# The S5 maps of a four-layer decoder on one core: other products on GpSimd, a layout made by transfers within DRAM, and loads of one megabyte

## The chip, the cores and the metric

The kernel runs on one core of one Trainium2 chip. The metric is the device time of one execution in microseconds (us). In the text, PE is TensorE, DVE is VectorE, ACT is ScalarE, POOL is GpSimd and SP is SyncE, as in the profile.

## The reference

256 tokens of 1024 channels pass four layers. Each layer is `h += rmsnorm(mixer(rmsnorm(h)))` and then `h += rmsnorm(mlp(rmsnorm(h)))`. The mixers are a gated MLP over chunks, a causal pooling, a latent attention and, in the last layer, S5, which the change concerns. All is float32.

```python
def s5_mixer(h, lam_re, lam_im, log_dt, b_re, b_im, c_re, c_im, d_skip, w_glu_a, w_glu_b):
    u = h.reshape(B_, S, S5_GROUPS, S5_GROUP_CH)          # 64 groups of 16 channels
    ...                                                    # ab = exp(lam dt), f = (ab - 1) / lam, complex
    bb = f * b                                             # 64 states x 16 channels per group
    bu = einsum('bsgc,gpc->bsgp', u, bb)
    x = scan(x = ab * x + bu)                              # over the tokens, complex
    y = einsum('bsgp,gcp->bsgc', x_re, c_re) - einsum('bsgp,gcp->bsgc', x_im, c_im) + d_skip * u
    y = gelu(y)
    return (y @ w_glu_a) * sigmoid(y @ w_glu_b)
```

## The kernel before

The eight sublayers (gated MLP, Mlp 0, pooling, Mlp 1, attention, Mlp 2, S5, Mlp 3) run one after the other, in blocks of 128 tokens. Every weight is split into two float32r parts, and a float32 product is three products of parts on PE (the helper at L296). SP loads the weights in pieces of 1 MB into three places called `raw`, and ACT (L338) and DVE (L339) split them into eight places called `w`. The order of the instructions on each engine is made by a scheduler that works on the program as it is traced.

**S5** works on chunks of 8 tokens, of which there are 32. Four matrices per group do the work: *f* takes a chunk's inputs to the state (`into`), *m* takes the inputs of a chunk to its outputs (`within`), the states between chunks are scanned on DVE (`scan`), and *e* takes the states to outputs (`out`). What depends on parameters only is made beside layers 1 to 3 by `Tables`, in 16 steps ("chunks of the maps") of two pairs of groups, and it goes to DRAM. S5 then loads these maps: four tiles of 16 groups for each of *f*, *m* and *e*, in `raw` and `w` places, followed by the two GLU weights.

**How the maps are made.** For each of the 16 steps POOL makes the products for *f* with the states in the rows (`ft`), and those for *e*. PE multiplies `ft` by the output matrices (`cb`), which gives *m* by lags between tokens (`pf<-ft,cb`, L296), and it transposes `ft` (L1676), so that the inputs stand in the rows. ACT takes both out of PSUM (L1664, L1678). Every second step PE transposes the lags (L1671), and DVE adds the skip term (`gs`, L1672). POOL issues the stores `d_f` and `d_e` of every step. At the end it stores `gs` to `d_g` 15 times (L1650), at places among zeros written earlier, so that one run of 512 B in `d_g` is a row of *m*.

**How they are loaded.** `load_map` (L1240) loads a tile of *m* by eight DMAs of 128 KB, and `load_out` (L1247) one of *e* by four DMAs of 256 KB. Both read runs of 512 B, on SP's queue, which is also the weights' queue. The *f* tiles are loaded by one DMA each (L113).

**The residual before S5.** S5 takes its tokens in another order. At the end of the attention `reorder` (L444) stores the two blocks of h to `d_h` (L451) and loads them back (L453), all on POOL's queue, behind the maps' last stores. The first readers of the loaded h are the sums of squares on ACT that give the norm factors of Mlp 2 (`junk<-h`, L352). They are wanted only at the end of Mlp 2, but ACT works in order.

Of the kernel before, what the change touches and what calls it, by code (L numbers as in the profile page):

```python
# [9 lines left out]
F32 = mybir.dt.float32  # L10
# [28 lines left out]
N_MAPS = 2  # L39
# [41 lines left out]
class Weights:  # L81
    """The weights in the order of their use, loaded and split ahead of it.

    A weight is the sum of two float32r parts, exactly; a piece is up to 1024 columns of them."""
# [34 lines left out]
    def skip_plain(self):  # L119
        """Past the plain tiles, of which those ahead are loaded where there is a place."""  # L120
# [8 lines left out]
    def ready(self, clock):  # L129
        """Whether the next piece can be split without a long wait for its place."""  # L130
# [34 lines left out]
    def take(self):  # L165
        """The next tile: its pairs, or itself where it is plain."""
# [12 lines left out]
    def free(self, n):  # L179
        """The last use of the next n pieces is emitted."""  # L180
# [9 lines left out]
class Core:  # L190
    """What the sublayers share: memory, the order of emission, norms and splits."""
# [40 lines left out]
    def chain(self):  # L232
        """A chain of short instructions, which the splits traced later don't get in between."""
# [6 lines left out]
    def after(self, first):  # L240
        """Instructions issued after those of first."""
# [6 lines left out]
    def behind(self):  # L248
        """Instructions that wait for the end of the last chain on their engine."""
# [8 lines left out]
    def tick(self, us):  # L258
        """The tensor engine got us of work: emit what runs beside it."""
# [21 lines left out]
    def run(self, units, side=()):  # L281
        """Emits the units (work of the tensor engine, us), and each of side (us, work) at its time among them."""
# [24 lines left out]
    def keep_warm(self, us, after=None):  # L307
        """Holds the tensor engine's clock up over a wait: us of products of zeros, after an instruction."""
# [9 lines left out]
    def acc(self):  # L318
        """[128 tok, 1024] in two banks."""
# [12 lines left out]
    def split(self, src, hi, lo, gain=None):  # L332
        """hi + lo = src, or src gain with [128, 1] of it."""
# [10 lines left out]
    def warm(self, func):  # L344
        """Has the table of func loaded."""
# [1443 lines left out]
```

## Time and profile before

| | |
|---|---|
| Time, median of 3 runs | 1138.8 us |
| The three runs | 1137.75, 1138.8, 1146.0 us |
| Span of the profiled execution (the only time listed for it) | 1139.8 us |
| PE, DVE, ACT, POOL busy | 90%, 64%, 49%, 30% of the span |
| Mean granted clock of PE | 0.955 |
| DMA | 213.84 MB, mean 188 GB/s |

The span is the time from the first to the last instruction of the one execution that was profiled, and it stands 1 us above the median of the runs. A busy share is an average over eight sublayers, so the stages that the change touches are read one by one: the making of the maps (about 215 to 580 us), the reordering of h (about 620 to 670 us) and S5 (about 818 to 935 us).

### The profile page before, as it was taken

The page shows a single profiled execution, that of the slowest core. Times are in us where ns is not written, and L with a number is a line of the kernel's source. Part 1 is how long each engine was busy: PE and PEld are TensorE (multiplying, and loading weights), DVE is VectorE, ACT ScalarE, POOL GpSimd, SP SyncE. Part 2 cuts the span into 40 slices and gives each one's busy share as a digit, 9 for nine tenths or more (in the row PEclk, how much of TensorE's full clock was granted, in tenths as well). Part 3 has the DMA queues.
Part 4 walks back from the last instruction along what each step waited for, and adds up shares of the span by engine and source line. Part 5 has one row for each costly group of instructions (what it writes and reads, how often), then busy time and mean ns, then how long its engine had stood idle before and what let it go on. Part 6 is the DMA issues. An engine that isn't in the chain of part 4 may idle for free.

```text
span 1139.8 us, 18030 instructions
## 1 busy us (share of the span) xinstructions
PE 1029.9 (90%) x7180; PEld 900.4 (79%) x7181; DVE 734.3 (64%) x1133; ACT 555.9 (49%) x841; POOL 343.8 (30%) x514
## 2 busy tenths in 40 slices
PE   7898999999589999997899969999962998999994
PEld 6886989997479888886688859989842787899984
DVE  5779999665686555657865655656574377645552
ACT  6956464454465434534565454545320466444541
POOL 4001002756898887889820100000000000000000
PEclk9999999999799999998899989999985799999998
DMA  9667476653565565545670966455599355555431
GB/s 330 219 222 265 167 250 204 220 184 112 189 236 164 207 206 183 171 146 174 212 220 27 253 190 215 165 206 179 178 176 264 113 179 190 185 184 199 171 112 37
DMA packets 93763, 213.84 MB, mean 188 GB/s; under 512 B 6272, under 2 KB 25984, under 8 KB 93168
## 3 DMA queue, kind: packets, MB, share of 16 engines
q1 hardware_dynamic: 83256, 182.73, 49.8%
q0 software_dynamic: 9872, 29.38, 8.4%
q8 instruction: 56, 0.92, 0.3%
q10 hardware_dynamic: 552, 0.59, 0.1%
q14 instruction: 27, 0.22, 0.1%
HBM read 197.53 MB, written 15.14 MB: 187 GB/s over the span
## 4 chain that ended last, share of the span: by engine, by line
PE 56%; POOL 14%; DMA 11%; issue 9%; DVE 6%; ACT 3%; SPq 0%; DVEq 0%; POOLq 0%; ACTq 0%
PE acc L296 29%; PE mm L296 25%; DMA w<-d_g 3%; DMA h<-d_h 2%; DMA raw<-in_a_w_in 2%; DVE w L339 2%; DMA d_e<-e 2%; POOL tmp L1530 1%; POOL tmp L1527 1%; POOL e L1531 1%; ACT junk L352 1%; POOL e L1528 1%; POOL ft L1531 1%; DVE w L337 1%; POOL ft L1528 1%
## 5 line engine op out<-in xcount | busy, mean ns | idle before, releaser
L339 DVE TENSOR_TENSOR w<-raw,w 128x1024 fp32r<-128x1024 f32 (+3 forms) x308 | 382.5, 1272 | 181.6 <-ACT w L338 180.1
L296 PE MATMUL acc<-w,h1hi 128*128 128x512 f32 (+2 forms) x1824 | 414.2, 350 | 23.6 <-ACT h1hi L338 12.4
L338 ACT ACTIVATE w<-raw 128x1024 fp32r<-128x1024 f32 (+3 forms) x308 | 313.2, 1044 | 243.1 <-PE acc L296 134.7
L296 PE MATMUL mm<-zhi,w 128*128 128x256 f32 x1920 | 357.3, 285 | 3.7 <-DVE s L820 2.3
L296 PEld LDWEIGHTS acc<-w,h1hi 128*128 128x128 f32 (+1 forms) x1824 | 252.5, 180 | 75.5 <-issue 14.4
L296 PEld LDWEIGHTS mm<-zhi,w 128*128 128x128 f32 x1920 | 303.3, 192 | 8.7 <-issue 2.8
L296 PE MATMUL mm<-zlo,w 128*128 128x256 f32 x960 | 273.0, 285 | 0.0
L296 PE MATMUL acc<-w,h1lo 128*128 128x512 f32 (+1 forms) x656 | 253.8, 390 | 1.3 <-DVE h1lo L339 1.3
L296 PEld LDWEIGHTS mm<-zlo,w 128*128 128x128 f32 x960 | 184.6, 192 | 2.3 <-issue 1.2
L296 PEld LDWEIGHTS acc<-w,h1lo 128*128 128x128 f32 x656 | 123.7, 188 | 28.5 <-DVE h1lo L339 2.3
L628 DVE TENSOR_TENSOR s<-s 128x512 f32<-128x512 f32 x56 | 42.0, 749 | 52.4 <-ACT s L627 52.4
L339 DVE TENSOR_TENSOR h1lo<-s,h1hi 128x512 fp32r<-128x512 f32 x60 | 51.2, 856 | 23.4 <-ACT h1hi L338 23.4
L627 ACT ACTIVATE s<-mm 128x512 f32<-128x512 f32 x56 | 33.3, 595 | 64.9 <-PE mm L296 63.2
L338 ACT ACTIVATE h1hi<-s 128x512 fp32r<-128x512 f32 x60 | 45.3, 756 | 25.3 <-DVE s L628 23.5
L1279 POOL MEMSET h1hi<- 128x32 f32 x2 | 0.3, 157 | 181.8 <-PE acc L296 181.8
L401 DVE TENSOR_TENSOR t<-acc,bc 128x512 f32<-128x512 f32 x28 | 19.0, 686 | 39.2 <-PE acc L296 39.2
L296 PE MATMUL mm<-w,zhi 128*128 128x512 f32 x128 | 40.2, 395 | 4.3 <-DVE zlo L339 3.8
L352 ACT ACTIVATE junk<-acc 128x512 bf16<-128x512 f32 x28 | 16.6, 594 | 53.6 <-DVE t L401 52.8
L296 PE MATMUL acc<-w,zhi 128*128 128x512 f32 (+2 forms) x128 | 38.3, 382 | 1.8 <-ACT w L336 1.8
L296 PE MATMUL pf<-ft,cb 128*32 128x128 f32 x128 | 20.8, 302 | 20.0 <-ACT f L1678 7.9
L352 ACT ACTIVATE junk<-h 128x512 bf16<-128x512 f32 x32 | 20.1, 628 | 26.4 <-DMA h<-d_h 16.6
L296 PEld LDWEIGHTS mm<-w,zhi 128*128 128x128 f32 x128 | 23.5, 188 | 10.0 <-DVE zlo L339 4.8
(279 smaller groups left out, 1153.1 us busy)
## 6 DMA issues: line engine op xcount, KB each, us to landing
raw<-in_w_up SPq DMA_DIRECT2D x64, 1024.0 KB, 5.4
raw<-in_w_down SPq DMA_DIRECT2D x64, 1024.0 KB, 5.1
bc<-in_norm_g POOLq DMA_DIRECT2D x15, 512.0 KB, 5.0
raw<-in_a_w_in SPq DMA_DIRECT2D x7, 1024.0 KB, 8.0
raw<-in_a_w_out SPq DMA_DIRECT2D x4, 1024.0 KB, 4.8
d_e<-e POOLq DMA_DIRECT2D x16, 256.0 KB, 3.9
d_f<-f POOLq DMA_DIRECT2D x16, 256.0 KB, 2.8
raw<-in_c_w_o SPq DMA_DIRECT2D x4, 1024.0 KB
```

The source lines that it names most:

```text
L296: return self.nc.tensor.matmul(out, lhsT, rhs, start=start, stop=stop)
L337: return i, nc.vector.scalar_tensor_tensor(lo, src, gain, hi.bitcast(F32), op0=ALU.mult, op1=ALU.subtract)
L338: i = nc.scalar.activation(hi, src, AF.Copy)
L339: return i, nc.vector.tensor_tensor(out=lo, in0=src, in1=hi.bitcast(F32), op=ALU.subtract)
L352: self.nc.scalar.activation(self.junk[:, 0:x.shape[-1]], x, AF.Square, scale=scale, bias=shift, accum_out=ss[:, i:i + 1])
L401: nc.vector.tensor_tensor(tn, zn, gn, op=ALU.mult)
L627: nc.scalar.activation(s, state[f], AF.Relu)
L628: nc.vector.tensor_tensor(s, s, s, op=ALU.mult)
L1527: eng.tensor_tensor(t, xi, yi, op=ALU.mult)
L1528: eng.tensor_tensor(out[0], out[0], t, op=ALU.subtract)
L1530: eng.tensor_tensor(t, xr, yi, op=ALU.mult)
L1531: eng.tensor_tensor(out[1], out[1], t, op=ALU.add)
```

## The change

POOL now makes *f* directly with the inputs in the rows. For this the powers of the decay must lie along a row, the same for the 16 channels. A new function `spread` computes them on DVE (six operations), has PE transpose them (four transposes), ACT copy them, and POOL store them to `d_pw` and copy them within DRAM to `d_pb`, by eight DMAs of 512 KB. Each step of the maps then loads its part of `d_pb` (`pb`) and the input matrices in that layout (`bt`), 256 KB each. The transposes of `ft` and of the lags are gone, with the copies behind them.

The lags are now products of `cb` and *e*, for two steps together, in four strips of 32 columns of PE. They come out as `[128, 128]`, ACT copies them, and `place` on POOL puts them, with zeros and the skip term, into rows that are stored to `d_lag`. When all steps are done, POOL issues four DMAs that copy *e* from `d_out` to `d_e` and eight that copy the lags from `d_lag` to `d_m`. Each is DRAM to DRAM, in runs of 512 B, 4 MB for each of the two. S5 loads *m* and *e* by one DMA of 1 MB per tile, as it loaded *f* before. The zeros of `d_g` and the 15 stores to it are gone. `N_MAPS`, the buffers of `e` and `cb` (before: of `ft` and `cb`), goes from 2 to 3. The rest of the diff takes out comments.

```diff
-N_MAPS = 2
+N_MAPS = 3
...
-        for c in range(4):
-            add(None, plain=True, ahead=True, shape=(16, 128), load=lambda t, c=c: self.load_map(t, c))
-        for c in range(4):
-            add(None, plain=True, ahead=True, shape=(16, 128), load=lambda t, c=c: self.load_out(t, c))
+        for maps in (k.d_m, k.d_e):
+            for c in range(4):
+                add(maps[:, 16 * c:16 * c + 16], plain=True, ahead=True)
...
+    def spread(self):
...
+        for n, (x, y, op) in enumerate(((fr, fi, ALU.subtract), (fi, fr, ALU.add))):
+            nc.vector.tensor_tensor(pw[:, n], turned(pr), wide(x), op=ALU.mult)
+            nc.vector.tensor_tensor(tmp[:, n], turned(pi), wide(y), op=ALU.mult)
+            nc.vector.tensor_tensor(pw[:, n], pw[:, n], tmp[:, n], op=op)
...
+            for n in range(4):
+                nc.tensor.transpose(ps[:, sl(n)], flat[:, sl(n)], k.ident)
+            nc.scalar.activation(s, ps, AF.Copy)
...
+        for i in range(8):
+            src = self.d_pw[:, i].rearrange("r h m -> r (h m)").partition_broadcast(16)
+            nc.gpsimd.dma_start(out=self.d_pb[16 * i:16 * i + 16].rearrange("l r h m -> l r (h m)"), in_=src)
...
     def maps(self):
...
-            self.cmul([v4(ft[:, r]) for r in range(2)], (wide(ov, 0), wide(ov, 1)), (pw(pr, last), pw(pi, last)), v4(tmp))
...
+            nc.gpsimd.dma_start(out=bt.rearrange("p r s m -> p (r s m)"), in_=a["k_bt"][ch])
+            nc.gpsimd.dma_start(out=pb.rearrange("p r s m -> p r (s m)"), in_=self.d_pb[:, :, ch])
...
+            nc.gpsimd.dma_start(out=self.d_out[:, qs], in_=e[:, :, :, 1:9].rearrange("p q r i c -> p q r (i c)"))
+            if made is not None:
+                self.place(lg, *made)
+                made = None
+            f = self.small("f", 4, 2, 64)
+            self.cmul([f[:, :, r] for r in range(2)], (pb[:, 0], pb[:, 1]), (bt[:, 0], bt[:, 1]), tmp.rearrange("p (s m) -> p s m", s=4))
+            nc.gpsimd.dma_start(out=k.d_f[:, 4 * ch:4 * ch + 4], in_=f.rearrange("p s r m -> p s (r m)"))
...
+            if ch % 2:
+                with k.tc.high_priority(offset=-LATER):
+                    made = ch // 2, self.lags((before, (cb, e)))
...
-                nc.gpsimd.dma_start(out=k.d_g[e, :, :, w + 3, o], in_=self.gs[16 * i:16 * i + 16])
...
+        for i, s in enumerate(TOKEN):
+            w = self.d_lag.rearrange("n (g c) f -> c (n g) f", c=16)[:, :, 256 * (s // 4) + 32 * (3 - s % 4):][:, :, 0:128]
+            nc.gpsimd.dma_start(out=k.d_m[16 * i:16 * i + 16], in_=w)
+        for r in range(2):
+            for g in range(2):
+                nc.gpsimd.dma_start(out=k.d_e[64 * r:64 * r + 64, g:64:2], in_=self.d_out[64 * g:64 * g + 64, :, r])
...
-                nc.tensor.transpose(ps[:, sl(2 * r + q)], ft[:, r, sl(q)], k.ident)
...
+    def place(self, lg, n, t):
...
+        nc.gpsimd.tensor_copy(v[:, 0, 0:4, 1], t[:, 1:8:2])
+        nc.gpsimd.tensor_copy(v[:, 0, 4:7, 1], t[:, 2:7:2])
+        for e in range(2):
+            nc.gpsimd.tensor_copy(v[:, e, 4:7, e], t[:, 1:6:2])
+        x = self.small("skip", 16)
+        nc.gpsimd.tensor_scalar(x, self.mask, self.skip[:, n:n + 1], None, op0=ALU.mult)
+        for e in range(2):
+            nc.gpsimd.tensor_tensor(v[:, e, 3, e], t[:, 0], x, op=ALU.add)
+        nc.gpsimd.dma_start(out=self.d_lag[n], in_=lg)
```

The scheduler orders the engines anew. On SP, the loads of S5 (`d_f`, `d_g` or `d_m`, and `d_e` are the maps in DRAM) stand so, before with a minus and now with a plus:

```order
 L113 DMA w<-d_f 128x2048
-L1240 DMA w<-d_g 16x16x128 x32
-L1247 DMA w<-d_e 64x8x128 x12
+L113 DMA w<-d_m 128x2048 x4
+L113 DMA w<-d_e 128x2048 x3
 L113 DMA raw<-in_d_w_glu_b 128x2x1024 x3
-L1247 DMA w<-d_e 64x8x128 x4
+L113 DMA w<-d_e 128x2048
 L113 DMA raw<-in_d_w_glu_b 128x2x1024
```

The order of the tiles is the same; 48 DMAs have become eight.

On POOL, before, the end of the maps and the reordering of h (`h_113` and `h_114` are the two blocks, `bc` are gains of norms, `d_tab` the frames of the scan):

```order
L1640 DMA d_e<-e 128x512
L328 DMA bc<-in_norm_g 128x1024
L1650 DMA d_g<-gs 1024x1x16 x15
L1679 DMA d_f<-f 128x512
L451 DMA d_h<-h_113 128x1024
L328 DMA bc<-in_norm_g 128x1024
L451 DMA d_h<-h_114 128x1024
L328 DMA bc<-in_norm_g 128x1024
L453 DMA h_113<-d_h 128x1x1024
L453 DMA h_114<-d_h 128x1x1024
L1260 DMA t<-d_tab 128x1024 x3
```

And now (`h_117` and `h_118` are the blocks):

```order
L1672 DMA d_e<-d_out 2048x128 x3
L1699 DMA d_lag<-lg 128x512
L451 DMA d_h<-h_117 128x1024
L1659 DMA d_f<-f 128x512
L328 DMA bc<-in_norm_g 128x1024
L451 DMA d_h<-h_118 128x1024
L328 DMA bc<-in_norm_g 128x1024
L1669 DMA d_m<-d_lag 1024x1x128 x8
L453 DMA h_117<-d_h 128x1x1024
L453 DMA h_118<-d_h 128x1x1024
L1246 DMA t<-d_tab 128x1024 x3
```

The eight copies to `d_m` stand between the stores of h and its loads, and the copies to `d_e` before the stores.

On ACT, before, the first readers of the loaded h among the work of Mlp 2 (`L599`, `L600` and `L627` are its activations, `h1hi` their high parts, `w<-raw` splits of weights):

```order
L599 ACTIVATE s<-mm 128x512
L338 ACTIVATE w<-raw 128x1024
L600 ACTIVATE s<-s 128x512
L352 ACTIVATE junk,ss<-h_113 128x512 x2
L352 ACTIVATE junk,ss<-h_114 128x512
L371 ACTIVATE sq<-v 128x1
L352 ACTIVATE junk,ss<-h_114 128x512
L338 ACTIVATE h1hi<-mm 128x32x16
```

And now:

```order
L338 ACTIVATE h1hi<-mm 128x32x16
L627 ACTIVATE s<-mm 128x512
L338 ACTIVATE h1hi<-s 128x512
L338 ACTIVATE w<-raw 128x1024 x2
L627 ACTIVATE s<-mm 128x512
L338 ACTIVATE h1hi<-s 128x512
L338 ACTIVATE w<-raw 128x1024 x4
L627 ACTIVATE s<-mm 128x512
L352 ACTIVATE junk,ss<-h_117 128x512 x2
L338 ACTIVATE h1hi<-s 128x512
```

The readers have moved behind the third activation at L627, which stood third behind them before.

## Rows read from the trace of the kernel before

**Rows 1.** The page, part 1, busy time of PE.

```profile
PE 1029.9 (90%) x7180; PEld 900.4 (79%) x7181; DVE 734.3 (64%) x1133; ACT 555.9 (49%) x841; POOL 343.8 (30%) x514
```

**Rows 2.** Timeline of SP: start, length, DMAs issued.

```profile
818.93 28.21 SPq L1240 DMA_DIRECT2D w<-d_g  x32
```

**Rows 3.** DMA queues, 818 to 850 us: packets, MB, share of 16 engines.

```profile
q1 hardware_dynamic: 8699, 5.18, 106.0%
```

**Rows 4.** DMA from 860 to 880 us, GB/s in slices of 0.5 us.

```profile
GB/s 266 258 210 202 217 287 219 223 243 231 258 215 256 369 418 426 442 377 418 401 418 418 410 442 410 368 318 202 202 206 252 243 246 216 145 223 346 172 205 287
```

**Rows 5.** Chain of waits, 800 to 935 us: start, length, what.

```profile
821.97 7.38 DMA w<-d_g
...
873.03 5.85 issue
...
897.67 36.33 PE acc L296 x160
```

**Rows 6.** Timeline of DVE in S5: start, length, work, idle before.

```profile
837.13 0.42 DVE L1277 TENSOR_TENSOR h1lo<-mm,t 128x256 f32<-128x256 f32 x1 [0.84 <-PE mm L1296]
...
852.43 0.42 DVE L1277 TENSOR_TENSOR h1lo<-mm,t 128x256 f32<-128x256 f32 x1 [2.85 <-PE mm L1296]
...
864.84 0.85 DVE L1277 TENSOR_TENSOR h1hi<-s 64x248 f32<-64x248 f32 x2
...
890.91 2.36 DVE L339 TENSOR_TENSOR w<-raw,w 128x1024 fp32r<-128x1024 f32 x2 [17.95 <-ACT w L338]
```

**Rows 7.** POOL from 350 to 545 us: busy, mean ns, idle before.

```profile
L1531 POOL TENSOR_TENSOR e<-e,tmp 128x256 f32<-128x256 f32 x9 | 11.5, 1281 | 0.6
...
L1526 POOL TENSOR_TENSOR ft<-bo,pr 128x256 f32<-128x256 f32 x9 | 7.8, 867 | 0.7 <-PE pf L1676 0.5
...
L1526 POOL TENSOR_TENSOR bo<-bo,v 128x32 f32<-128x32 f32 x9 | 4.6, 515 | 12.8 <-DMA bo<-in_k_bc 12.8
```

**Rows 8.** Stores of e, L1640: ns min/median/max, first and last start.

```profile
L1640 POOL DMA_DIRECT2D d_e<-e x15: 542/601/606, 237.4 to 561.9; - x15
```

**Rows 9.** What PE waited for, 225 to 635 us: total, times, longest.

```profile
PE pf L296 <- ACT f L1678: 7.9, 1, 7.9
PE pf L296 <- POOL ft L1528: 6.5, 2, 5.2
```

**Rows 10.** Timeline of PE: four transposes of ft, one of lags.

```profile
562.77 0.27 PE L1671 MATMUL pf<-ident,lags 128*128 128x128 f32 x1
...
563.88 0.60 PE L1676 MATMUL pf<-ident,ft 128*128 128x128 f32 x4
```

**Rows 11.** Timeline of POOL, reordering of h.

```profile
621.65 0.55 POOL L451 DMA_DIRECT2D d_h<-h  x1 [41.31 <-DVE h L405]
...
636.39 0.53 POOL L451 DMA_DIRECT2D d_h<-h  x1 [4.25 <-DVE h L405]
...
640.51 1.40 POOL L453 DMA_DIRECT2D h<-d_h  x2 [2.38 <-DMA d_h<-h]
```

**Rows 12.** DMA queue of POOL, 637 to 641 us.

```profile
q0 software_dynamic: 248, 0.95, 65.3%
```

**Rows 13.** DMA queue of POOL, 564 to 580 us.

```profile
q0 software_dynamic: 494, 1.27, 40.1%
```

**Rows 14.** Both DMA queues, 645 to 655 us.

```profile
q0 software_dynamic: 523, 1.32, 99.0%
q1 hardware_dynamic: 41, 0.08, 5.9%
```

**Rows 15.** Timeline of ACT in Mlp 2.

```profile
661.26 0.63 ACT L352 ACTIVATE junk<-h 128x512 bf16<-128x512 f32 x1 [14.34 <-DMA h<-d_h]
...
686.09 0.60 ACT L627 ACTIVATE s<-mm 128x512 f32<-128x512 f32 x1 [3.19 <-PE mm L296]
```

**Rows 16.** Windows, 660 to 665 us: busy by engine, PE clock, DMA.

```profile
660.00:665.00 5.00, 0.00 (x0) 0.00 (x0) 0.21 (x1) 1.47 (x5) 0.00 (x0) 0.63 0.88 304
```

**Rows 17.** What PE waited for, 600 to 720 us.

```profile
PE acc L296 <- ACT h1hi L338: 10.9, 2, 10.2
```

More of the change, by code (lines that the diff above doesn't have):

```diff
@@ L1413, in __init__ @@
         k.d_f = k.dram.tile([128, 64, 128], F32, name="d_f")
-        k.d_e = k.dram.tile([128, 16, 2, 2, 128], F32, name="d_e")
-        k.d_g = k.dram.tile([2, 16, 64, 8, 2, 16], F32, name="d_g")
+        k.d_m = k.dram.tile([128, 64, 128], F32, name="d_m")
+        k.d_e = k.dram.tile([128, 64, 128], F32, name="d_e")
+        self.d_pw = k.dram.tile([2, 8, 16, 256], F32, name="d_pw")
+        self.d_pb = k.dram.tile([128, 2, 16, 256], F32, name="d_pb")
+        self.d_lag = k.dram.tile([8, 128, 512], F32, name="d_lag")
+        self.d_out = k.dram.tile([128, 32, 2, 128], F32, name="d_out")
     def small(self, name, *shape):
@@ L1549, in recurrence @@
         self.mask = load("k_mask", 16)
-        self.skip = load("d_skip", 64)
-        zero = self.wide()
-        nc.gpsimd.memset(zero, 0.0)
-        for n in range(4):
-            part = self.k.d_g.rearrange("b c g w o e -> (b c g) (w o e)")[512 * n:512 * n + 512]
-            nc.gpsimd.dma_start(out=part.rearrange("(p n) f -> p (n f)", p=128), in_=zero)
+        self.skip = load("d_skip", 8)
         v = [self.small(f"v{n}", 32) for n in range(6)]
@@ L1604, in recurrence @@
         yield 0
+        yield from self.spread()
         dec = self.wide().rearrange("p (q j) -> p q j", j=32)
@@ L1633, in maps @@
                 hs = slice(64 * g, 64 * g + 64)
-                nc.gpsimd.tensor_copy(cv[hs, 0, :, g], bv[hs, 2])
-                nc.gpsimd.tensor_scalar(cv[hs, 1, :, g], bv[hs, 3], -1.0, None, op0=ALU.mult)
-            e = self.small("e", 2, 2, 128)
-            first = slice(0, 8)
-            self.cmul([e[:, :, r].rearrange("p q (i c) -> p q i c", c=16) for r in range(2)], (wide(bv, 2), wide(bv, 3)), (pw(pr, first), pw(pi, first)), v4(tmp))
-            nc.gpsimd.tensor_scalar(e[:, :, 1], e[:, :, 1], -1.0, None, op0=ALU.mult)
@@ L1640, in maps @@
-            nc.gpsimd.dma_start(out=k.d_e[:, ch], in_=e)
+                nc.gpsimd.tensor_copy(cb[hs, :, :, g], ov[hs])
+            wide = lambda n: bv[:, n, :, None, :].to_broadcast([128, 2, 8, 16])
+            pw = lambda t: t[:, qs, 0:8, None].to_broadcast([128, 2, 8, 16])
+            self.cmul([e[:, :, r, 1:9] for r in range(2)], (wide(2), wide(3)), (pw(pr), pw(pi)), tmp.rearrange("p (q i c) -> p q i c", q=2, c=16))
+            nc.gpsimd.tensor_copy(e[:, :, :, 0], bv[:, 2:4].rearrange("p n q c -> p q n c"))
@@ L1641, in maps @@
             yield MAPS_US
-            with k.tc.high_priority(offset=-LATER):
-                self.turned(ch, cv, ft)
+            if ch % 2:
+                with k.tc.high_priority(offset=-LATER):
+                    made = ch // 2, self.lags((before, (cb, e)))
+            before = cb, e
             yield 0
-        for i in range(8):
-            lag = 7 - TOKEN[i]
-            at = [(0, lag, 0), (1, lag, 1)] if lag < 4 else []
-            at += [(0, lag - 4, 1)] if lag else []
-            for e, w, o in at:
-                nc.gpsimd.dma_start(out=k.d_g[e, :, :, w + 3, o], in_=self.gs[16 * i:16 * i + 16])
+        self.place(lg, *made)
@@ L1673, in turned @@
-        ps = k.pf.tile([128, 512], F32, name="pf")
-        for q in range(2):
-            for r in range(2):
-                nc.tensor.transpose(ps[:, sl(2 * r + q)], ft[:, r, sl(q)], k.ident)
-        f = self.small("f", 4, 128)
-        nc.scalar.activation(f.rearrange("p g (r m) -> p r g m", r=2), ps.rearrange("p (r g m) -> p r g m", r=2, g=4), AF.Copy)
-        nc.gpsimd.dma_start(out=k.d_f[:, 4 * ch:4 * ch + 4], in_=f)
+        for r in range(2):
+            for n, (cb, e) in enumerate(pairs):
+                for q in range(2):
+                    k.mm(ps[sl32(2 * n + q), 0:128], cb[:, r, q].rearrange("p g c -> p (g c)"), e[:, q, r, 0:8].rearrange("p i c -> p (i c)"), r == 0, r == 1)
```

70 lines of the change are left out of this document (31 added, 39 removed).

## The prediction

> **What bounds the kernel now.** The page gives PE 90% of the span [rows 1], so the first question in each stage is what PE waits for when it does not run. I read the profile in this order: the waits by engine, then the chain of waits of the two stages in which PE stands longest, then the queues behind them.
>
> The first stage is S5. SP issues the 32 loads of *m* over 28.21 us [rows 2]. In that stretch the weights' queue fills the DMA engines, a share of 106% of them, but moves only 5.18 MB in 32 us, 162 GB/s [rows 3]. Some 20 us later, on the same queue, slices of half a microsecond reach 418 to 442 GB/s while a GLU weight is loaded [rows 4]. So this is not a full memory but many short runs. The chain of waits shows what it costs: from 821.97 us it goes through loads of *m*, then through gaps of over 5 us ("issue") before PE's products with *e*, and the dense projection begins only at 897.67 us [rows 5]. The scan on DVE does not set that end: it runs from 837.13 to 865.69 us and stands only 2.85 us in between [rows 6]. After it DVE waits, 17.95 us the last time, for weights that come late.
>
> The second stage is the reordering of h. POOL issues the loads at 640.51 us [rows 11], ACT gets h at 661.26 us after 14.34 us of waiting [rows 15], and PE stands 10.2 us [rows 17]; its clock falls to its lower level in that stretch (0.63 mean over 5 us) [rows 16].
>
> The third is the making of the maps beside layers 1 to 3. PE is mostly busy there; it waits for the maps' own steps 7.9 and 6.5 us in all [rows 9].
>
> **A, making the maps.** Gone from PE are 64 transposes of `ft`, 16 times four at 0.60 us or 9.6 us [rows 10], eight of the lags at 0.27 us, about 2 us [rows 10], and the waits for *f* and `ft`. Added are four transposes. The lag products stay 64, in narrower strips. PE is the engine that sets the pace between those waits, so some 9 us of this would count on the path, the rest being hidden in the waits. ACT and DVE lose 16 evictions and eight sums and gain six small operations, which lie beside PE's work: I cost them at nothing, and it stays so unless DVE's work for `spread` delays a norm.
>
> But PE can only get ahead as far as POOL does. A step on POOL keeps its twelve wide operations, of 0.87 us (product) to 1.28 us (sum) [rows 7]. It gains two loads at 0.6 us each [rows 8], one small copy, and in every second step `place`, seven small operations and a store. It loses two small operations and half a skip product. With 0.5 us for a small operation [rows 7] that is 1.2 + 0.5 + 2.1 - 1.25 = about +2.5 us. Before, the stores of *e* come every 23.2 us over 14 intervals (237.4 to 561.9 us) [rows 8], longer waits included; 2 us of that I put down to those longer waits. So I take about 23.5 us after. The first *f* also starts late, since it waits for the powers. `spread`'s transposes stand in PE's order where the trace has about 250 us, then come `d_pw`, 4 MB of copies to `d_pb` and the load of `pb`. At 2.75 to 5 us per MB (below) that is 272 to 285 us. With *e* of the second step some 14 us later and 14 more steps, the last *e* is ready at 615 to 628 us. PE wants it about 8 us ahead of the store of the second block of h, 636.39 us before [rows 11], and 9 us earlier if it has gained those: at about 620. So 0 to 8 us of the gain are lost again. **A = -4 us**, from -9 to +12, where the upper end is 1.5 us per step that POOL is slower than I think.
>
> **B, the reordering of h.** This is the price of the layout in DRAM. The 8 MB of copies to `d_e` and `d_m` go into POOL's queue ahead of the loads of h. Behind them on POOL wait only h, the scan's frames (not wanted before S5) and two gains. What a megabyte costs there no row of before shows, since no DRAM to DRAM copy ran. The nearest rows of POOL's queue bound it. Without company, 0.95 MB took 65.3% of 4 us: 2.75 us per MB of the engines' time [rows 12]. The 15 stores of lags, in short runs, took 40.1% of 16 us for 1.27 MB: 5.05 us [rows 13]. The load of h, whose neighbouring rows lie 32 KB apart in DRAM, took 99% of 10 us for 1.32 MB: 7.5 us [rows 14]; in that time the weights' queue got 0.08 MB. The 512-byte runs of the old S5 loads make 6.5 us [rows 3]. I take 5.05, the row of POOL's queue with short runs, and keep 2.75 and 7.5 as ends.
>
> [...]
>
> The copies can start when the last *e* is stored, about 625 us. At 5.05 us per MB they hold the engines 40 us if alone, about 55 beside the weights, so to about 680, and h lands at about 684. When is it wanted? ACT's readers of h have moved behind the third L627. Before, that stood at 686.09 us [rows 15], after some 12.6 us of standing and slow clock. So it is wanted at about 673, or 670 with A, and PE has work for 6 us more. PE then stands about 11 us instead of 10.2, plus the clock's 2, and some 4 us go where the weights' queue gets too little: **B = +4 us**. At 2.75 h lands by about 655 and nothing waits: -12. At 7.5 the copies end at 685 or later and the weights stop, with at most 7 MB in their places (some 38 us of work): PE stands about 30 us, +20.
>
> **C, S5.** The maps' loads become eight of 1 MB, in runs as long as those of `d_f`. At 300 to 400 GB/s 8 MB need 20 to 27 us from 818.3 us, so *m* is there by about 834 and *e* by 848 (the last tile waits for its place, not for time). Then nothing in `within` or `out` waits for a transfer, and DVE's scan sets the end: it starts at 837.13 as before and, without the 2.85 us [rows 6], ends at 862.8. All splits of the GLU weights on DVE stand behind it in its new order. Five splits at 1.2 us [rows 6] and two of activations lie ahead of the low parts that the projection needs, so it runs densely from about 870.5 instead of 897.67 us [rows 5]. That would be -27. If the loads run at 250 GB/s, the last tile of *e* comes near 872 and the gain is 18. **C = -25 us**, from -18 to -28. The projection itself takes its 36.33 us as before [rows 5], and what follows moves with it.
>
> **Sum.** Against the profiled execution: 1139.8 - 4 + 4 - 25 = 1114.8. That execution lies 1 us above the median, which I leave in the rounding: 1115 us.
>
> **The rivals.** *No wait for h.* If the copies cost 2.75 us per MB, PE stands nowhere for h: 1139.8 - 4 - 12 - 25 = 1099. For it: plain transfers on this queue do it [rows 12]. Against: both ends are DRAM and the runs are short.
>
> *The copies crowd out h and the weights.* This is the one that ends slower. Place: POOL's queue from 625 us until h lands. It costs PE everything past about 676 us, and it decides where the copies take over 10 us per MB: then 8 MB end at 705, PE restarts at about 712, stands 36 with 4 more for weights and clock, and the 29 us of A and C are eaten. At 15 us per MB, twice the slowest row, they end at 745 and the time is about 1139.8 - 29 + 65 = 1176. For it speaks [rows 14], where 1 MB of h with its 32 KB step took nearly all engines and left the weights 0.08 MB. Against: no row shows 10. A milder form, 7.5 us per MB, gives 1139.8 - 4 + 20 - 25 = 1131.
>
> *GpSimd comes late.* If a step takes 25 us instead of 23.5, the last *e* comes at 650 us, PE waits some 20 to 30 us for the lag products that stand in its order, though h's own wait then falls into it: 1139.8 + 12 - 3 - 18 = 1131.
>
> *The loads gain nothing.* S5 stays as long as it is and the time is 1139.8 - 4 + 4 = 1140. The scan's end at 865.69 [rows 6], 32 us ahead of the projection, and the waits for `w<-d_g` in the chain [rows 5] speak against it. [...]
>
> **How the numbers follow.** A measurement of this kernel can tell about 1% from no change, that is 11.4 us, so faster ends at 1127 and slower begins at 1150. Forecast (1103 to 1127) 0.44, faster. No wait for h 0.20, faster. Copies at 7.5 us per MB 0.08, same. Copies past 10 us per MB 0.14, slower. GpSimd late 0.10, same. Loads gain nothing 0.04, same. So faster 0.64, same 0.22, slower 0.14. The range goes down to 1094 (no wait for h, with A and C at their good ends less a little) and up to 1150, where the slower rival begins; outside lie that rival and a few hundredths below.
>
> **What would show it.** In the changed profile I expect: no load in S5's chain of waits, SP's maps issued in under 10 us, the scan's end at about 863 less the shift before it, the projection right behind it. At the reordering: the copies to `d_m` landing 40 to 55 us after the first copy to `d_e`, an ACT wait for `h<-d_h`, PE idle there 8 to 15 us. In the maps: no `f<-pf`, steps of about 23.5 us on POOL, PE waits for `e` or `cb` of a few microseconds near the end. The forecast is wrong if PE stands over 30 us between 630 and 720 us, if POOL's last map comes after 645 us, or if the projection of S5 begins more than 15 us behind the scan.

## The result

The changed kernel takes 1121.99 us in the median of four runs (1119.85 to 1123.67), the kernel before 1141.32 us in four runs beside them. The ratio is 0.9833, with a 95% interval of 0.9802 to 0.9864: faster, by 19 us. The forecast was 1115 us. The profiled executions differ as much as the medians do, 1139.8 us against 1120.5 us, so their traces can be set side by side. Each trace is cut here at three places that both kernels have: the first block of h after layer 3, the start of S5 (the 34 products of zeros that PE makes ahead of its first products, line 296 on `pf`), and the dense projection of S5.

| | before | after | moved by |
|---|---|---|---|
| first block of h added (DVE `h`, line 405) | 619.92 | 619.73 | -0.2 |
| start of S5 (PE `pf`) | 825.76 | 823.04 | -2.5 more |
| dense projection (PE `acc` x160) | 897.67 | 877.56 | -17.4 more |
| end of the span | 1139.8 | 1120.5 | +0.8 more |

So in this pair of traces terms A and B together brought some 3 us, where they were forecast to cancel, and C brought 17.4 instead of 25. How far one pair can be trusted is taken up with the experiments. PE is busy for 91% of the span, where it was 90% [rows 1].

**S5.** The timeline of SP of the kernel after (start, length, DMAs issued), answering to [rows 2], and the DMA view from 815 to 860 us, answering to [rows 3] and [rows 4]; its first line has slices of 1.1 us, its second the weights' queue with packets, MB and share:

```profile
816.20 5.08 SPq L113 DMA_DIRECT2D w<-d_m  x4
821.64 1.68 SPq L113 DMA_DIRECT2D w<-d_e  x3
...
840.42 0.34 SPq L113 DMA_DIRECT2D w<-d_e  x1
```

```profile
GB/s 0 138 328 430 444 408 430 444 408 430 444 411 397 317 433 408 422 451 408 422 408 419 411 397 426 422 422 441 441 277 51 15 0 0 15 0 0 15 0 0
...
q1 hardware_dynamic: 2112, 12.58, 68.4%
```

The 28.21 us of issuing *m* became 5.08 us, and the queue that gave 162 GB/s with full engines runs at over 400 GB/s in nearly every slice until everything is there at about 848 us. The chain of waits shows what is left, answering to [rows 5], and the timeline of DVE the start and the end of the scan, answering to [rows 6]:

```profile
823.04 7.50 PE pf L296 x34
...
844.79 4.30 issue
849.08 1.93 PE acc L1331 x128
851.01 1.80 issue
...
877.56 36.33 PE acc L296 x160
```

```profile
834.41 0.42 DVE L1263 TENSOR_TENSOR h1lo<-mm,t 128x256 f32<-128x256 f32 x1 [0.84 <-PE mm L1282]
...
859.37 0.85 DVE L1263 TENSOR_TENSOR h1hi<-s 64x248 f32<-64x248 f32 x2
```

No load stands in the chain any more. But it doesn't go through the scan either: it goes along PE, a batch of products and a gap ("issue": PE waits for nothing that the profile shows), again and again, and ends 17 us behind the scan. The timeline of PE (start, length, work, idle before) shows the batches more closely:

```profile
852.81 1.94 PE L1331 MATMUL acc<-w,zlo 128*32 128x32 f32 x128 [1.80 <-issue]
856.54 1.19 PE L1331 MATMUL acc<-w,zlo 128*32 128x32 f32 x73 [1.79 <-issue]
857.53 0.95 PE L296 MATMUL acc<-w,h1hi 128*32 128x32 f32 x55
860.14 1.94 PE L296 MATMUL acc<-w,h1hi 128*32 128x32 f32 x127 [1.67 <-issue]
```

From 842 us on a gap comes after every 128 products (transposes counted), also where a batch runs over the border from one map to the next: 73 of the map `m` and 55 of the map `e` make 128. A product has a weight load beside it (256 products and 255 loads from 852 to 860 us), so that is 256 instructions of PE.

**The maps and h.** The timeline of POOL, answering to [rows 8] and [rows 11]: the first *f*, the last three stores of *e*, and the second block of h:

```profile
269.72 0.72 POOL L1516 TENSOR_TENSOR f<-pb,bt 128x256 f32<-128x256 f32 x1 [3.74 <-DMA pb<-d_pb]
...
576.59 0.82 POOL L1653 DMA_DIRECT2D d_out<-e  x1
...
598.71 0.83 POOL L1653 DMA_DIRECT2D d_out<-e  x1
...
612.60 0.82 POOL L1653 DMA_DIRECT2D d_out<-e  x1
...
645.02 0.54 POOL L451 DMA_DIRECT2D d_h<-h  x1 [12.09 <-DVE h L405]
```

PE's waits from 225 to 720 us (total, times, longest), answering to [rows 9] and [rows 17], the rows of over 3 us for `t` (what the norms give) and for *e*:

```profile
PE mm L428 <- DVE t L418: 16.1, 3, 8.9
PE pf L296 <- POOL e L1518: 12.1, 6, 5.4
PE mm L428 <- DVE t L1041: 4.6, 2, 3.7
...
PE pf L296 <- POOL e L1652: 3.2, 1, 3.2
```

The wait for h is gone, and one of 8.9 us for the norm ahead of Mlp 2 stands in its place. The DMA view from 625 to 665 us (queues; then issues with KB each and median us to landing), answering to [rows 12] to [rows 14], and the timeline of ACT, answering to [rows 15], show why:

```profile
q0 software_dynamic: 2661, 9.86, 67.8%
q1 hardware_dynamic: 2060, 5.14, 34.3%
...
d_m<-d_lag POOLq DMA_DIRECT2D x8, 512.0 KB, 13.8
...
raw<-in_w_up SPq DMA_DIRECT2D x3, 1024.0 KB, 14.5
```

```profile
640.38 1.06 ACT L338 ACTIVATE w<-raw 128x1024 fp32r<-128x1024 f32 x1 [7.50 <-DMA raw<-in_w_up]
641.35 0.19 ACT L371 ACTIVATE sq<-v 128x1 f32<-128x1 f32 x1
...
686.87 0.63 ACT L352 ACTIVATE junk<-h 128x512 bf16<-128x512 f32 x1 [2.91 <-DMA h<-d_h]
```

POOL's queue, most of it the copies, took 67.8% of 40 us for 9.86 MB, 2.75 us per MB (0.678 x 40 / 9.86), and h came in time. Yet they held up a weight of Mlp 2: it took 14.53 us from its issue at 625.77, where the page has 5.5 as the median of 64. ACT stood 7.50 us for it, with the norm's small operation `sq` queued behind; DVE, PE and the second store of h waited in turn. PE's clock fell to 0.50, where [rows 16] has 0.63 (windows; the last three columns are clock, DMA share and GB/s):

```profile
640.00:645.00 5.00, 0.00 (x0) 0.00 (x0) 3.42 (x8) 3.21 (x5) 0.00 (x0) 0.50 1.02 412
645.00:650.00 5.00, 4.52 (x17) 4.06 (x18) 4.14 (x6) 1.79 (x3) 4.30 (x7) 0.50 1.03 406
```

### The profile page after: what moved, and what is told of

Its sections match the earlier page's. It is cut to its first block, busy times and chain, and to the rows that moved or that the text cites. A ratio compares the mean times of both kernels' runs of the same rounds, so it can differ in the third digit from the quotient of the medians.

```text
span 1120.5 us, 17841 instructions
## 1 busy us (share of the span) xinstructions
PE 1020.5 (91%) x7112; PEld 898.2 (80%) x7113; DVE 741.5 (66%) x1131; ACT 546.2 (49%) x818; POOL 377.2 (34%) x588
## 4 chain that ended last, share of the span: by engine, by line
PE 59%; POOL 17%; DVE 9%; DMA 6%; issue 4%; ACT 4%; SPq 0%; DVEq 0%; POOLq 0%; ACTq 0%
PE acc L296 29%; PE mm L296 27%; DVE w L339 3%; POOL tmp L1520 2%; DMA raw<-in_a_w_in 2%; POOL tmp L1517 2%; DMA raw<-in_w_down 2%; DMA raw<-in_w_up 1%; DMA d_f<-f 1%; ACT w L338 1%; ACT junk L352 1%; DVE h L405 1%; PE pf L296 1%; POOL f L1516 1%; POOL e L1652 1%
## 5 line engine op out<-in xcount | busy, mean ns | idle before, releaser
L627 ACT ACTIVATE s<-mm 128x512 f32<-128x512 f32 x56 | 33.4, 596 | 72.6 <-PE mm L296 70.6
L339 DVE TENSOR_TENSOR h1lo<-s,h1hi 128x512 fp32r<-128x512 f32 x60 | 54.0, 901 | 21.4 <-ACT h1hi L338 21.4
L296 PE MATMUL mm<-w,zhi 128*128 128x512 f32 x128 | 42.8, 417 | 2.0 <-DVE zlo L339 1.5
L428 PE MATMUL mm<-ident,t 128*128 128x128 f32 x86 | 14.7, 312 | 24.5 <-DVE t L418 19.9
L428 PEld LDWEIGHTS mm<-ident,t 128*128 128x128 f32 x86 | 11.4, 159 | 27.7 <-issue 26.0
L328 POOL DMA_DIRECT2D bc<-in_norm_g x15 | 8.3, 556 | 75.0 <-DVE t L401 25.2
## 6 DMA issues: line engine op xcount, KB each, us to landing
raw<-in_a_w_in SPq DMA_DIRECT2D x7, 1024.0 KB, 10.5
```

What stands on the lines that cost most here:

```text
L296: return self.nc.tensor.matmul(out, lhsT, rhs, start=start, stop=stop)
L339: return i, nc.vector.tensor_tensor(out=lo, in0=src, in1=hi.bitcast(F32), op=ALU.subtract)
L428: self.nc.tensor.transpose(ps[:, k * 128:(k + 1) * 128], z[:, k * 128:(k + 1) * 128], self.ident)
L627: nc.scalar.activation(s, state[f], AF.Relu)
```

## The experiments

Two questions: what in the loads of S5 was worth 17 us, and what held the rest back (C); and what the copies cost ahead of S5 (A, B). The theory for C was that short runs made the old loads slow; the rival, first put when the trace of after was read, that PE's instructions come too slowly where its products are small. Each experiment's ratio is taken to runs of the kernel before on the same chip (their medians are 1138.69 to 1140.82 us). Profiles of kernels with the same work ahead of S5 start S5 at times up to 10 us apart, so for S5 the stage's own length is compared: from PE's first `pf` in S5 to the end of the span. It is 314.0 us before and 297.5 after. Other traces show how far to trust one such length: with the loads of after it is 294.1 to 296.3 us in the three runs on the copies below (`b_`), but with the old loads 307.5 us in `h_before_late`.

### Loads alone: c_bigloads

The kernel before, its maps in S5 loaded by one DMA per megabyte, all of them from `d_f`, so that *m* and *e* are not the right ones:

```diff
-        for i, s in enumerate(TOKEN):
-            src = self.k.d_g[s // 4, :, 16 * c:16 * c + 16, 3 - s % 4:7 - s % 4].rearrange("c g w o e -> c g (w o e)")
-            self.nc.sync.dma_start(out=t[16 * i:16 * i + 16], in_=src)
+        self.nc.sync.dma_start(out=t, in_=self.k.d_f[:, 16 * c:16 * c + 16])
```

> The kernel before, in which each tile of m and e for S5 is loaded by one DMA of 1 MB from d_f (long runs), so that the products of S5 use other numbers; the making of the maps, the 15 stores to d_g and the reordering of h stay as before. Theory: the long runs alone give the gain that the changed kernel shows in S5, where the dense projection came 17 us earlier against the stage's own start; so 16 to 20 us faster than before, with h's wait of about 14 us on ACT unchanged and gaps of 1.7 to 2.5 us after every 128 small products on PE, no longer 3 to 6 us. Rival: the gain needs the new making of the maps (fewer waits ahead of S5), then less than 8 us.

1126.79 us, ratio 0.9885 (0.9838 to 0.9932), 13 us where 16 to 20 were expected. The stage is 295.8 us long, 18 shorter than before: the loads alone give all that S5 gained in the change, and the new way of making the maps has no part in it. The gaps on PE are the same as after. PE's waits from 815 to 905 us, of before, of after and of `c_bigloads`:

```profile
PE acc L1345 <- issue: 18.8, 5, 5.2
PE acc L296 <- issue: 11.2, 4, 5.9
```

```profile
PE acc L1331 <- issue: 10.3, 4, 4.3
PE acc L296 <- issue: 5.9, 4, 2.4
```

```profile
PE acc L1340 <- issue: 10.7, 4, 4.3
PE acc L296 <- issue: 5.5, 4, 1.9
```

All three have one more gap of 1.3 us, ahead of the first products of S5, and none has a load in its list, though the chain of before passes through loads [rows 5]. So the old loads cost PE most of their price through these gaps: 30.0 us became 16.2. While the loads keep the DMA engines full a gap lasts up to 5.9 us before and 4.30 us after (until 849.08 us, the loads ending at about 848); right behind them it is 1.7 to 1.8 us.

### Short runs: c_shortruns, c_slices, c_slices_short

Of the kernel after, each megabyte by two DMAs of every second group: runs of 512 bytes, but 128 partitions.

```diff
+        for g in range(2):
+            self.nc.sync.dma_start(out=t[:, g:16:2], in_=maps[:, 16 * c + g:16 * c + 16:2])
```

> The changed kernel, in which each tile of m and e for S5 is loaded by two DMAs, of its even and of its odd groups, so in runs of 512 B, from the new d_m and d_e. Theory: the length of the runs is what costs; loads at about 160 GB/s, S5 longer by 14 to 20 us, in all 1136 to 1142 us, about the time before. Rival: the number of DMAs on SP is what cost (48 before, 8 after, 16 here); then at most 4 us over the changed kernel.

1121.36 us, ratio 0.9816 (0.977 to 0.9863), stage 295.6: as fast as after. My theory fell. With runs of 512 bytes the queue still moved 345 to 348 GB/s in 15 of the 16 slices from 823 to 841 us (slices of 1.1 us from 815 us), and that is enough:

```profile
GB/s 0 15 0 109 175 430 337 346 348 347 346 347 347 422 346 345 348 348 345 348 348 346 347 362 316 340 274 306 408 430 404 408 426 390 358 342 220 45 15 0
```

What is left of the old loads is their shape: for *m*, 32 DMAs of 16 partitions and 128 KB each. So the next two runs take that shape and set it apart from the runs:

```diff
+        for i in range(8):
+            self.nc.sync.dma_start(out=t[16 * i:16 * i + 16], in_=maps[16 * i:16 * i + 16, 16 * c:16 * c + 16])
```

> The changed kernel, in which each tile of m and e for S5 is loaded by eight DMAs of 16 partitions and 128 KB, in runs of 8 KB. The run of two DMAs per tile in runs of 512 B took the changed kernel's time at about 347 GB/s, so the short runs by themselves are not what made the old loads slow. Theory now: a DMA that covers 16 partitions only (one per DMA engine) is slow into SBUF whatever its runs; about 160 to 200 GB/s between 820 and 850 us, S5 longer by 10 to 16 us, 1131 to 1138 us. Rival 1: it takes both, few partitions and short runs; then 1119 to 1125 us here. Rival 2: the row pitch in d_g in DRAM (64 KB) made them slow; then 1119 to 1125 us here too.

```diff
+        g0 = min(16 * c, 32)
+        for i in range(8):
+            self.nc.sync.dma_start(out=t[16 * i:16 * i + 16], in_=maps[16 * i:16 * i + 16, g0:g0 + 32:2])
```

> The changed kernel, in which each tile of m and e is loaded by eight DMAs of 16 partitions with 16 runs of 512 B, 1 KB apart in DRAM, the shape of the old loads of m, but from rows 32 KB apart instead of 64; every second group of a stretch of 32 is taken, so the products of S5 use other numbers. If few partitions with short runs are the cause: about 160 GB/s, 1131 to 1140 us. If the pitch of d_g was: over 300 GB/s, 1119 to 1125 us.

1125.54 us (0.9882, 0.9849 to 0.9916) and 1126.22 us (0.9896, 0.9851 to 0.9941), the stage 305.4 us in both, 8 longer than after. The rate is the one expected, the time is less than the 1131 us expected at the least: by the ratios 6 to 7 us over the changed kernel, with intervals that touch its own. The loads are back in the chain of waits of `c_slices` (start, length, what), and the rate from 815 to 860 us is the same for runs of 8 KB (`c_slices`, first line of the DMA view) as for runs of 512 bytes (`c_slices_short`, second; slices of 1.1 us):

```profile
818.12 6.09 DMA w<-d_m
...
824.23 7.45 DMA w<-d_m
```

```profile
GB/s 189 160 197 153 197 153 193 131 320 259 189 175 189 168 204 175 189 197 160 204 182 189 197 182 204 197 182 197 189 189 189 182 204 189 211 168 208 251 411 426
```

```profile
GB/s 348 162 189 185 188 185 193 210 283 232 193 190 186 191 185 193 189 185 200 179 185 184 172 202 161 163 211 168 209 170 191 194 168 205 175 185 195 167 232 375
```

So it is DMAs of 16 partitions and 128 KB that hold the rate to some 185 GB/s (the mean of the slices below 230), whatever their runs. Issuing is not the limit, since the weights' queue takes 96.4% of the DMA engines' time in `c_slices`. But few partitions and small DMAs come together here; no run has small DMAs over 128 partitions, so that it is the partitions is argued, not shown. How the 16 partitions fall on the 16 DMA engines, of which the expectation speaks, is not shown either: the views have only the mean of the engines. PE pays in its gaps again, 24.5 us in `c_slices` against 17.5 after (815 to 905 us):

```profile
PE acc L296 <- issue: 12.1, 4, 3.8
PE acc L1335 <- issue: 8.2, 3, 3.0
PE mm L296 <- issue: 4.2, 2, 2.9
```

The old loads themselves run once more in `h_before_late` below, whose S5 is that of the kernel before. From 809 to 841 us, the 32 us that [rows 3] has from 818 us, its weights' queue moves 193 GB/s:

```profile
q1 hardware_dynamic: 10719, 6.18, 107.7%
```

With a stage of 307.5 us there, the shape of the DMAs accounts for all but 2 us of what the old loads cost there. Why the trace of before has 162 GB/s and 314.0 us with the same loads stays open.

### Fewer, wider products: s5_wideprod, s5_wide

PE's gaps follow its products in number, one after every 128 from 842 us on (above). If instructions come too slowly, a quarter of the products with four times the columns must take the gaps away. The first kernel only changes the products; the second also lays out y, the transposes behind it and the rows of the GLU weights to match.

```diff
-                    for s in range(4):
-                        m = sl32(s)
-                        x = nc.tensor.matmul(ys[c][m, sl32(i)], u[:, 16 * c + i], t.raw[:, i, m], start=not i, stop=False)
+                    x = nc.tensor.matmul(ys[c][sl32(i % 4), sl(i // 4)], u[:, 16 * c + i], t.raw[:, i], start=i < 4, stop=False)
...
-                nc.tensor.transpose(ps[:, sl(2 * n + b)], yt[:, b, sl(2 * c + n)], k.ident)
+                nc.tensor.transpose(ps[:, sl(s)], yn[:, 2 * s + b, sl(c // 2)], k.ident)
```

> The changed kernel, in which within and out in S5 make one product of 128 columns per group instead of four of 32 columns to four strips, so a quarter of the instructions for the same columns; the results land at other places of y. Theory: after the change neither the loads (done at 847 us) nor the scan (done at 860 us) ends S5, but PE's supply of instructions: after every 128 products with their 128 weight loads it stands 1.7 to 2.4 us; with a quarter of the instructions these gaps go and the projection follows the scan at 866 to 870 us instead of 877.6, 7 to 11 us faster. Rival: the gaps belong to the tiles (a wait for a load or a place that the profile does not show), one per tile as before; then within 2 us of the changed kernel.

> The changed kernel with within and out as one product of 128 columns per group, as in the run that tested PE's supply of instructions, now with y laid out for it: the transposes of y take one block of tokens per turn, and the rows of the GLU weights are given in the order that results. The transposes, splits and products behind are as many as before. Theory: the whole gain of that run stays, 1101 to 1108 us. Rival: the last turns, which now come both behind the last tile, take it back in part; 1108 to 1115 us.

1104.9 us (0.9687, 0.964 to 0.9734) and 1105.65 us (0.9699, 0.9655 to 0.9742); the stage is 285.3 and 285.05 us, 12 shorter than after, where 7 to 11 were expected. PE's waits of `s5_wide` from 815 to 900 us, its scan's end and dense projection, and the queue that the view calls `instruction` in the 30 us up to the dense projection, first of `s5_wide` (830 to 860 us), then of the kernel after (850 to 880 us):

```profile
PE acc L296 <- DVE h1hi L1263: 7.2, 3, 3.7
...
PE mm L296 <- issue: 1.3, 1, 1.3
...
PE acc L1330 <- issue: 1.0, 1, 1.0
```

```profile
852.81 0.86 DVE L1263 TENSOR_TENSOR h1hi<-s 64x248 f32<-64x248 f32 x2
```

```profile
859.55 36.32 PE acc L296 x160
```

```profile
q8 instruction: 3, 0.05, 0.7%
```

```profile
GB/s 22 0 0 0 0 22 0 0 0 0 22 0 0 0 0 22 0 0 82 235 404 404 295 0 0 0 0 22 0 0 0 22 71 55 393 431 410 38 120 164
...
q8 instruction: 7, 0.11, 1.6%
```

The gaps fell from 17.5 us (10.3, 5.9 and 1.3) to 2.3, and PE now waits for the scan (7.2 us), as the prediction had it: the projection is dense from 859.55 us, 5.9 us behind the scan's end at 853.67. The view of after even shows the beat: where nothing else moves, one slice in five (3.75 us) has 22 GB/s, 16 KB, and the batches of 128 products start 3.6 to 3.7 us apart. That the gaps are bound to the count of products is shown. That PE waits there for instructions still to be loaded is argued from this beat, and from the gaps' length while loads fill the DMA engines (up to 4.30 us, against 1.7 to 1.8 behind them), not shown: no run changed how instructions come. Not all 12 us are gaps either, since the wide products take 1.06 us of PE for 32 where four times as many narrow ones take 1.93.

### The copies and the wait for h: b_nocopies, b_nocopies_late, h_before_late, b_copies_behind

First the kernel after without its twelve copies, S5 reading `d_f` in their place:

```diff
-        for maps in (k.d_m, k.d_e):
+        for maps in (k.d_f, k.d_f):
...
-            nc.gpsimd.dma_start(out=k.d_m[16 * i:16 * i + 16], in_=w)
...
-                nc.gpsimd.dma_start(out=k.d_e[64 * r:64 * r + 64, g:64:2], in_=self.d_out[64 * g:64 * g + 64, :, r])
```

> The changed kernel without the twelve copies from d_lag and d_out to d_m and d_e; S5 loads all its tiles from d_f, so that its products of m and e use other numbers. Theory: the copies cost what the wait for h cost before, now as a late weight load: ACT waited 7.5 us for raw<-in_w_up and PE stood 8.85 us at 636 to 645 us with its clock halved for some 8 us; without them 9 to 13 us faster than the changed kernel, PE standing under 2 us between 620 and 700 us. Rival: the place of the readers of h on ACT and POOL's late end matter more; h comes at about 660 us either way and the time falls by less than 4 us.

1122.04 us (0.9827, 0.9775 to 0.9879): nothing gained, where 9 to 13 us were expected. Without the copies the order puts the readers of h back where they stood before, and the old wait returns. Timeline of ACT and PE's waits from 600 to 720 us:

```profile
660.95 0.63 ACT L352 ACTIVATE junk<-h 128x512 bf16<-128x512 f32 x1 [15.21 <-DMA h<-d_h]
```

```profile
PE acc L296 <- ACT h1hi L338: 12.0, 2, 11.3
```

So in the next two the readers of h on ACT are kept late by hand (behind group 2 of the second Mlp): in the kernel without copies, and in the kernel before.

```diff
-            side = [(5.0, self.factors)] if g == 1 else ()
+            side = [(5.0, self.factors)] if g == (2 if self.i == 2 else 1) else ()
...
+        if self.i == 2:
+            last = [i for i in k.traced() if i.engine == mybir.EngineType.Activation][-1]
+            with k.after([last]):
+                self.r = [k.factor(b) for b in range(NB)]
+            return
```

> The changed kernel without the copies within DRAM (S5 loads d_f for all its tiles, other numbers) and with the readers of h on ACT forced behind the second group of Mlp 2. Without the copies alone the scheduler put the readers back to their early place, and PE stood 11.35 us for h, so that run lost by the one what it won by the other. Theory: copies and the wait for h cost about 9 to 12 us each, one in the place of the other; with neither, 1108 to 1113 us, PE standing under 3 us in one piece between 630 and 720 us. Rival: PE stands there for weights anyway, since the loads of h starve the weights' queue; then over 1116 us.

> The kernel before with one thing changed: the readers of h on ACT stand behind the second group of Mlp 2 instead of the head. Theory: the 14 us wait of ACT goes and with it PE's 10.2 us and the slow clock, 9 to 13 us faster than before (1127 to 1131 us), so that this part of the change needs nothing of the maps. Rival: while POOL's queue loads h the weights' queue gets nothing, and PE stands for weights instead; less than 5 us.

1112.58 us (0.9773, 0.9722 to 0.9823) and 1131.33 us (0.9928, 0.9887 to 0.9968). With neither copies nor the wait for h, PE waits for nothing longer than this from 600 to 780 us (`b_nocopies_late`):

```profile
PE mm L428 <- DVE t L418: 1.0, 1, 1.0
```

So the copies as they stand cost some 7 to 10 us (ratios of 0.9833 and 0.9773, spans of 1120.5 and 1110.7 us), and the late readers alone are worth 8 to 9.5 us in the kernel before, its S5 starting at 816.34 instead of 825.76. In the change the one pays for the other. Last, the copies put behind the loads of h, with late readers:

```diff
-            nc.gpsimd.dma_start(out=self.h[b], in_=in_chunks(d)[b])
+            last = nc.gpsimd.dma_start(out=self.h[b], in_=in_chunks(d)[b])
+        with self.after([last.ins]):
+            self.arrange()
```

> The changed kernel with the twelve copies within DRAM behind the loads of h on POOL's queue, and the readers of h on ACT forced behind the second group of Mlp 2. Theory: the copies hurt where they fall on the head of Mlp 2, in which the weights' places are emptied fast; 30 us later the weights' queue can do with its share, and the time is that of the kernel without copies and with late readers, 1110 to 1116 us. Rival: 8 MB of copies take the same from the weights wherever they lie; PE stands 8 us or more in one piece between 665 and 710 us, 1118 to 1124 us.

1109.21 us (0.9728, 0.967 to 0.9786), and S5 starts at 810.47 us, 12.6 earlier than after (3.4 of it ahead of h). All 8 MB are still copied, and PE waits for nothing over 1.1 us from 600 to 780 us. It was the place of the copies that cost, not their bytes.

### Together: both, both_lags

`both` is `s5_wide` with `b_copies_behind`. `both_lags` also makes the lag products of a pair of maps one step later, so that PE waits less for *e*:

```diff
-                    made = ch // 2, self.lags((before, (cb, e)))
+                    made = pending[0], self.lags(pending[1])
+            if ch % 2:
+                pending = ch // 2, (before, (cb, e))
```

> The two together: copies behind h with late readers, and the products of 128 columns in S5. The stages lie 100 us apart, so the gains should add: 8 us and 15 us under the changed kernel, 1093 to 1102 us. Rival: S5 that starts earlier meets frames and maps that land late; above 1104 us.

> As the run before, and the lag products of two steps of the maps are given to PE one step later (N_MAPS stays 3, since a fourth buffer finds no room). PE waited 15 us in all for e from POOL in the changed kernel. Theory: those waits are lost time on PE, half of them go, 4 to 9 us faster than the run before. Rival: POOL, which makes a step in some 22 us, has too few buffers and waits for PE instead, or PE's waits fall elsewhere; within 3 us of the run before.

1102.8 us (0.9685, 0.9634 to 0.9736) and 1103.78 us (0.9665, 0.9598 to 0.9732). Both beat the changed kernel, but not `s5_wide` alone by more than the runs scatter. Added up, the two gains over the changed kernel would give `both` a ratio of 0.9594. Its profiled execution, the fastest of four, shows no such shortfall: S5 starts 15.3 us earlier than after and its stage is 9.7 us shorter (287.8 us), 25.0 in all, where the traces of the two have 12.6 and 12.4. Why the other executions are slower stays open; no trace shows one of them. The later lag products showed no gain that can be measured.

## Why the prediction was right, and where it was off

**The sign and the place were right.** The change is faster, nearly all of it in S5, through the loads of the maps. The step that was off is the size of C, "DVE's scan sets the end", with 25 us forecast and 17.4 measured. The prediction saw the gaps called issue in the chain [rows 5] and took them all for the loads' price. They were so in part: the trace of before has 30.0 us of them from 815 to 905 us (18.8 and 11.2); with full-rate loads 16.2 remain (10.3 and 5.9), and `c_bigloads` has the same. PE, not the scan, sets the end. The size of C is itself known only roughly: from the start of S5 to the dense projection it is 71.9 us before and 54.5 after, but 65.0 in `h_before_late`, which has the old loads too; by that trace C is 10.5. Either way it is outside the -18 to -28 that the prediction gave. The scan ran as forecast, 25.8 us from its start, without standing. The mark set for a wrong forecast, a projection more than 15 us behind the scan, was reached: it is dense 17 us behind it. `s5_wide` shows the forecast's own case, 5.9 us behind.

**The cause given for the slow loads was wrong.** "Not a full memory but many short runs" is refuted by `c_shortruns`. At 128 partitions 512 B gave 347 GB/s, less than the 400 and more of runs of 8 KB but more than twice the 162 [rows 3]. That the loads became fast all the same was luck as far as the reason goes: the change also made them 128 partitions wide and 1 MB long.

**A, -4 forecast, about 0 in this pair of traces, some -5 over all traces.** In this pair the first block of h comes 0.2 us earlier. From 225 to 620 us PE works 6.2 us less (363.67 us before, 357.47 after) and stands as much longer. Not for POOL: it waits 15.3 us for *e* (12.1 and 3.2), where it waited 14.4 for *f* and `ft` [rows 9]. Its waits for `t` on DVE grew from 2.0 to 11.9 us (7.3 at line 418, 4.6 at line 1041), while one of 5.6 us for a norm on ACT went. So what offsets the gain is the term that the prediction put at nothing, the work on DVE, by the very condition that it named, a delayed norm; what delays DVE is not shown.

But the pair is not typical. The five other runs with the same work ahead of S5 (`c_shortruns`, the two of slices, the two wide ones) have that block of h at 611.7 to 621.8 us, with after 616.0 in the mean; the three with the old maps (before, `c_bigloads`, `h_before_late`) have it at 619.9 to 623.1, 621.5 in the mean. By these -4 was about right. POOL's steps were 22.5 us in the mean (the stores of *e* come from 297.4 to 612.6 us, 14 intervals; the last two are 22.1 and 13.9), quicker than the 23.5 forecast. The first *f* came at 269.72 (272 to 285 forecast) and the last *e* at 612 (615 to 628).

**B, +4 forecast, -2.5 measured, by other steps than forecast.** From h to the start of S5 it is 203.3 to 204.6 us in five of the six traces with the changed work (208.9 in the sixth), 205.8 in before and 206.7 in `c_bigloads`, so the sign holds in five of six. The price of the copies was the low end, 2.75 us per MB; the row taken, 5.05, was of stores from SBUF in short runs [rows 13], and of the rows shown the plain transfer [rows 12] came closest. The copies to `d_m` were issued up to 654 us and h was there at 686.87, a wait of 2.91 us on ACT and none on PE. That made the rival "no wait for h" right in its premise, but not in its time: its -12 assumed that nothing waits in h's place. The 4 us set aside for a starved weights' queue were 8.9 us on PE and 10 us at a clock of 0.50 (640 to 650 us), since one late weight held up a norm behind it on ACT. The rival "copies crowd out h and the weights" named this mechanism, at prices that it didn't reach.

**The sum.** With the terms of this pair, 1139.8 - 0.2 - 2.5 - 17.4 + 0.8 = 1120.5. The errors of A (+3.8), B (-6.5) and C (+7.6) partly cancelled, so that the total came within 7 us of the forecast is in part luck. A and C differ by 5 us and more from trace to trace, so their shares are rough.

## What to carry to other kernels

Before loads are called slow by their runs, look at how many partitions and bytes one DMA covers, and test the runs apart from them: with runs of 512 bytes, DMAs of 16 partitions and 128 KB gave 185 GB/s here, of 128 partitions and 512 KB 347. An idle time that the profile puts down to "issue" was a limit of its own here, and its count was that of PE's products, one gap after every 128 of 15 ns: where products are short, count them. Faster transfers took away only what the full queue had added to it (30.0 to 16.2 us), and wider products nearly all of the rest (17.5 to 2.3 us, both with the gap of 1.3 ahead of the first products). And bulk copies that nobody wants soon belong behind the transfers that somebody does: the same 8 MB cost 7 to 10 us ahead of h and the next weights, and left PE no wait over 1.1 us behind them.

## What the runs showed of the hardware

- In the S5 of the kernel after, PE stood 1.7 to 4.3 us (once 0.2) after every 128 products of 15 ns with their weight loads, 256 instructions, whichever map they were for, longest (4.30 us) while loads filled the DMA engines: 17.5 us in all, with the gap of 1.3 ahead of the first products. Where nothing else moved, the queue `instruction` moved 16 KB every 3.75 us, about one per batch (850 to 862 us). With products of 33 ns, a quarter as many, one such gap of 1.0 us was left in `s5_wide`.
- DMAs of 16 partitions and 128 KB gave some 185 GB/s with runs of 8 KB and of 512 bytes alike; of 128 partitions, 347 GB/s with 512 bytes (512 KB a DMA) and over 400 with 8 KB (1 MB a DMA).
- Copies within DRAM took 2.75 us per MB on POOL's queue beside the weights (625 to 665 us), and 2.6 from 655 to 665 us (66.7% of 10 us for 2.56 MB), when the copies to `d_m`, whose reads step by 32 KB, stood next in that queue. That is less than half of the 7.5 us that the load of h took [rows 14]. While they ran, the two queues together moved 376 GB/s in the mean, and a weight of 1 MB took 14.53 us to land.
